# GpSimd issues the direct tiles' stores, the gates' convolution gets a low rank, a third place for sums of values, and sums in DRAM closer together

## The chip, the core and the metric

The kernel runs on one core of one Trainium2 chip. Its time is the device time of one launch in microseconds (us); three launches gave 1119.26, 1120.39 and 1120.42, so the median is 1120.39 us. The core has a matrix engine (PE, with its weight loads shown as PEld), a vector engine (DVE), a scalar engine (ACT), GpSimd (POOL) and a queue engine (SP) that does no arithmetic here but issues nearly all transfers. Each engine runs its own list of instructions in order; an instruction that waits holds up everything behind it on that engine.

## What is computed

One layer of a bidirectional encoder over 256 positions and 16 meta tokens, in float32: two groups of attention heads, an output projection, and then a gated MLP whose gate passes a convolution of width 3 over the positions. The change touches the MLP alone:

```python
def conv_glu(x, w_gate, w_up, conv_w, conv_b, w_down):
    L = x.shape[1]
    g = x @ w_gate
    u = x @ w_up
    pad = CONV_W // 2
    gp = jnp.pad(g, ((0, 0), (pad, pad), (0, 0)))
    gc = conv_b
    for i in range(CONV_W):
        gc = gc + conv_w[i] * gp[:, i:i + L]
    return (jax.nn.silu(gc) * u) @ w_down
...
        h = h + mix @ w_out[l]
        h = h + conv_glu(rmsnorm(h, ffn_norm_g[l]), w_gate[l], w_up[l], conv_w[l], conv_b[l], w_down[l])
    return h[:, N_META:]
```

D_MODEL is 2048 (16 tiles of 128), D_FF is 5632 (44 tiles).

## The kernel before

**Weights.** All weights are float32 and are streamed from DRAM in pieces of up to 128x1024. SP issues the load of a piece into a buffer (`raw`, `more_raw`, and late in the kernel `halves`, which is the same pool of buffers; all loads have line 540). ACT writes a rounded copy of the piece, `whi` (L247), DVE writes the remainder `wlo = raw - whi` (L251), and PE makes each product in parts: the high half of the weights with the high and the low half of the data, and the low half of the weights with the high half of the data (L710 to L712, L2026 and L2027, L287). There are four `whi` and four `wlo` buffers, so DVE can be at most four pieces ahead of PE.

**The MLP** begins about 396 us into the span. Gate and up tiles come in pairs. `gated` (called when a gate tile's products are complete) multiplies by the row's scale and then makes the convolution: one activation on ACT, two SCALAR_TENSOR_TENSOR on DVE (L259), a SiLU on ACT. `tile_up` multiplies the up tile by the gate, and `finish_value` stores the value as two halves in `act`. Five groups of four up tiles (QUADS) are made by a scheme with seven products in place of eight; it needs sums of the data, which for some are kept in `act` (`near`) and for others come from DRAM (`s_up`) into one of two buffers `sin` (the slots `s_parts`), and sums of the weights, which DVE makes. The down projection has three parts: 512 columns by the scheme with narrow products ("mid", `w_down_m`, its sums of values saved in `s_down` and loaded again through `s_parts`), 1024 columns by the scheme with wide products (`w_down_s`), and four tiles of 128 columns made directly (`w_down`). A direct tile has six pieces of up to 8 blocks each. Of its 22 pairs' weight sums the wide part takes one or two of three from DRAM (`early`): GpSimd adds them there with accumulating transfers (L779), between about 400 and 830 us.

**A direct tile's end** (`down_out`): for the first three, ACT copies two halves out of PSUM, GpSimd makes three additions and products (L275), and SP issues the store (L2015), behind whatever GpSimd still has to do. For the last tile DVE makes two operations. `mid_out` and `scheme_out` end the other two parts: DVE combines the seven products, ACT scales, GpSimd adds the residual (L275), SP stores (L2181, L2222).

**The order of everything** is made by a planner in the kernel: each piece of work is a coroutine that asks for an engine with a cost in ns, and `Flow.run` always takes the one that can start first, ties and ranks by `order()` (a lower rank goes first). So a changed cost or rank moves instructions on every engine. The table `work` sets the order of PE's weight pieces; `TAIL` says how the last six pieces of mid ("m") and the first pieces of the direct tiles ("d") alternate before the wide part begins.

Of the kernel before, what the change touches and what calls it, by code (L numbers as in the profile page):

```python
# [34 lines left out]
KC = D_MODEL // P  # L35
# [23 lines left out]


THIRD = 2
MID_SUMS = 0
EARLY_PACE = 18000.0
LANDING = 2600.0
BEHIND = 4
MID_LEAD, TAIL = 4, "mmdmmdddmmddd"
LAST = FC // 2 - 1


# [145 lines left out]
def encoder_block(ctx: ExitStack, tc: tile.TileContext, io):  # L215
# [15 lines left out]
    def size(ap):  # L231
        n = 1
        for s in ap.shape[1:]:
            n *= s
        return n
# [7 lines left out]
    def ACT(out, in_, f, **kw):  # L243
        ns = (51 if in_psum(in_) else 93) + 0.833 * size(in_)
        ns += 93 * (columns(kw.get("scale")) + columns(kw.get("bias")) > 0)
        yield "act", ns + 113 * ("accum_out" in kw)
        nc.scalar.activation(out, in_, f, **kw)  # L247
# [9 lines left out]
    def STT(out, a, s, b, op0, op1):  # L257
        yield "dve", 68 + 62 * columns(s) + 1.04 * size(out)
        nc.vector.scalar_tensor_tensor(out, a, s, b, op0, op1)  # L259
# [11 lines left out]
        nc.vector.reciprocal(out, a)  # L271

    def PTT(out, a, b, op):
        yield "pool", 90 + 2.7 * size(out)
        nc.gpsimd.tensor_tensor(out, a, b, op)  # L275

    def cost(l, r):
# [28 lines left out]
    def one(slots):  # L306
        (t,) = yield slots, 1
        return t
# [1585 lines left out]
    def gated(f, gate):  # L1894

        yield ev_mlp
        gs = yield from one(mts)

        yield from TT(gs[:, : SEQ + 1], gate[:, : SEQ + 1], s_2[:, : SEQ + 1], ALU.mult)
        fl.put(acc, gate)  # L1900
        gc = yield from one(mts)
        g_ = gc[:, :SEQ]
        yield from ACT(
            g_, gs[:, 1 : 1 + SEQ], AF.Identity, scale=vec("conv0", f), bias=vec("conv_b", f)
        )
        yield from STT(g_, gs[:, :SEQ], vec("conv1", f), g_, ALU.mult, ALU.add)
        yield from STT(
            gc[:, 1:SEQ], gs[:, : SEQ - 1], vec("conv2", f), gc[:, 1:SEQ], ALU.mult, ALU.add
        )
        yield from ACT(gs[:, :SEQ], g_, AF.Silu)  # L1910
        fl.put(mts, gc)
        gates[f] = gs
        fl.set(ev_gate[f])
# [50 lines left out]
    def save_sums(dst, saved, parts, release):  # L1964
        yield "sp", 600
        load(dst, parts, saved, nc.sync)
        fl.cur.t = saved.time
        if release:
            fl.put(combined, parts)

# [27 lines left out]
    def down_out(m, ps):  # L1998
        o = yield from one(mts)
        o_ = o[:, :SEQ]  # L2000
        if m < KC - ST - 1:
            t = yield from one(mts)
            yield from ACT(o_, ps[:, :SEQ], AF.Copy)
            yield from ACT(t[:, :SEQ], ps[:, SEQ:], AF.Copy)
            fl.put(acc, ps)
            yield from PTT(o_, t[:, :SEQ], o_, ALU.add)
            fl.put(mts, t)
            yield from PTT(o_, o_, s_2[:, :SEQ], ALU.mult)
            yield from PTT(o_, o_, hT[ST + m][:, :SEQ], ALU.add)
        else:  # L2010
            yield from TT(o_, ps[:, :SEQ], s_2[:, :SEQ], ALU.mult)
            fl.put(acc, ps)
            yield from TT(o_, o_, hT[ST + m][:, :SEQ], ALU.add)
        yield "sp", 600
        nc.sync.dma_start(io["outT"][:, m, :], o_)  # L2015
        fl.cur.t += 4000.0
        fl.put(mts, o)

# [74 lines left out]
    def scheme_products(p, r):  # L2093
        if r.last and not r.wide and p is r.pieces[0]:
            fl.spawn(reserve())
        if r.of != "up":
            yield ev_act[2 * r.g]
            yield ev_act[2 * r.g + 1]
        for i, n in enumerate(p.products):
            if r.first:  # L2100
                yield from sums7_bank(r, n)
            if n in (1, 2, 4):
                k, h = {1: (0, 0), 2: (1, 0), 4: (1, 1)}[n]
                k += 2 * r.g
                A = hl[k] if r.of == "up" else act[:, k]
                a = [A[:, j, h * P : (h + 1) * P] for j in range(2)]
            else:
                yield r.ev_S
                if r.near:
                    r.S = near[r.g]  # L2110
                o = P * {6: 0, 7: 1, 3: 2, 5: 3}[n]
                a = [
                    r.S[:, j * PW // 2 + o : j * PW // 2 + o + P].bitcast(F32R) for j in range(2)
                ]
            t = slice(i * r.q, (i + 1) * r.q)
            for s, ev in zip(p.parts, p.ready):
                if s.start < t.stop:
                    yield ev

            j = r.order.index(n)  # L2120
            start = r.first and (r.wide or j % 2 == 0)
            stop = r.last and (r.wide or j % 2 == 1 or j == 6)
            yield from MM(product3(sums7[n], a, (p.hi[:, t], p.lo[:, t]), start, stop))
        finished()
        if p is r.pieces[-1]:
            if not r.near:
                fl.put(s_parts, r.S)
            elif r.last_near:
                fl.set(ev_far[r.g])
            if r.last:  # L2130
                P7 = dict(sums7)
                sums7.clear()
                if r.of == "down":
                    fl.spawn(scheme_out(P7))
                elif r.of == "mid":
                    fl.spawn(mid_out(r.order, P7, dict(sum_banks)))
                else:
                    fl.spawn(quad_out(r.quad, r.order, P7, dict(sum_banks)))
# [33 lines left out]
    def mid_out(order, P7, b):  # L2172
        out = yield from reserved()
        U = quarters_of(out)
        yield from seven(order, P7, b, U)
        for i in range(2):
            for j in range(2):
                yield from ACT(U[i][j], U[i][j], AF.Copy, scale=s_2t[:, i : i + 1])
                yield from PTT(U[i][j], U[i][j], res[SL // (2 * P) + j][:, i, :], ALU.add)
            yield "sp", 600  # L2180
            nc.sync.dma_start(io["out"][i][:, SL:], out[:, i * SM : (i + 1) * SM])  # L2181
        fl.cur.t += 4000.0
        fl.put(raws, out)

# [26 lines left out]
    def scheme_out(sums7):  # L2211
# [4 lines left out]
        def done(i, j):  # L2216
            for k in range(2):
                o = C[i][j][:, k * 2 * P : (k + 1) * 2 * P]
                yield from ACT(o, o, AF.Copy, scale=s_2t[:, i : i + 1])
                yield from PTT(o, o, res[2 * j + k][:, i, :], ALU.add)  # L2220
            yield "sp", 600
            nc.sync.dma_start(io["out"][i][:, j * SL // 2 : (j + 1) * SL // 2], C[i][j])  # L2222

# [22 lines left out]

    fl.spawn(split_x(), 2)
    fl.spawn(split_hi(), lambda: -1 if 16 < n_split[0] < at[0] + 2 else 2)
    fl.spawn(split_lo(), lambda: -1 if 16 < n_split[1] < at[0] + 2 else 2)
    fl.spawn(square_x(), lambda: 3 if sq_n[0] < 10 else 0)  # L2250
    fl.spawn(sum_x(), 3)
    fl.spawn(scale_x())
# [165 lines left out]
```

## Time and profile before

| what | value |
|---|---|
| three launches | 1119.26, 1120.39, 1120.42 us |
| the profiled execution's own time | 1118.23 us |
| its span | 1116.4 us |
| matmuls | 8164 |
| PE's share of the span | 99% |
| DVE's share | 91% |
| ACT's share | 68% |
| POOL's share | 14% |

The span runs from the first to the last instruction. The busy time of PE is the union of its matmuls, whose ends are modelled and overlap, so a matmul that runs at a lower clock still counts as busy. The granted clock (PEclk) is 1.00 at full speed. In the timeline a row is: start in us, duration in us, engine, line, operation, out<-in, shape, how many were merged, and in brackets the idle time of the engine before it and what ended that.

### The profile page before, as it was taken

To read this page: it belongs to the slowest core of one execution; us is meant where nothing else is said; L and a number is where in the kernel's file an instruction comes from. 1 tells how busy PE (TensorE), PEld (TensorE's weight loads), DVE (VectorE), ACT (ScalarE), POOL (GpSimd) and SP (SyncE) were. 2 spreads that over 40 slices of the span, in tenths; PEclk is the share of its full clock that TensorE was granted. 3 is DMA by queue.
4 is the path that set the end of the run, shared out by engine and by line. 5 is a ranking of instruction groups with operands and counts; after the bars stand their busy time and mean duration, and the time that the engine had idled before them with its cause. 6 is when DMAs were issued, how large, how long until landed. Compare 5 with 4: busy or idle time off the path is not lost.

```text
span 1116.4 us, 22345 instructions
## 1 busy us (share of the span) xinstructions
PE 1099.7 (99%) x8164; PEld 1048.3 (94%) x8164; DVE 1012.1 (91%) x1918; ACT 754.1 (68%) x1518; POOL 157.6 (14%) x216
## 2 busy tenths in 40 slices
PE   9999999999999999999999999999999999998998
PEld 9999999999999999999999999999999999786877
DVE  8979888888879899999999999999999999997996
ACT  8688979897647776556665665665566565665564
POOL 3211222122333400000000000000000000304022
PEclk9999999999999999999999999999999999998999
DMA  8654435344655798787868778898898889797881
GB/s 325 196 167 133 153 111 165 132 149 150 228 182 167 210 335 273 252 244 233 295 193 250 254 245 282 268 284 274 302 345 305 277 302 334 249 333 260 295 302 51
DMA packets 82887, 265.35 MB, mean 238 GB/s; under 512 B 9304, under 2 KB 13400, under 8 KB 82776
## 3 DMA queue, kind: packets, MB, share of 16 engines
q1 hardware_dynamic: 79320, 255.00, 66.4%
q0 software_dynamic: 3168, 8.65, 4.9%
q8 instruction: 64, 1.05, 0.4%
q14 instruction: 47, 0.39, 0.1%
q10 hardware_dynamic: 288, 0.27, 0.1%
HBM read 245.39 MB, written 35.13 MB: 251 GB/s over the span
## 4 chain that ended last, share of the span: by engine, by line
PE 64%; DVE 19%; DMA 7%; ACT 6%; issue 3%; POOL 1%; SPq 0%; DVEq 0%; ACTq 0%; POOLq 0%
PE bank L287 17%; PE bank L712 11%; PE bank L710 11%; PE bank L711 11%; DVE wlo L251 10%; PE bank L2026 7%; PE bank L2027 4%; DVE raw L251 3%; ACT whi L247 3%; DVE mt L251 2%; PE bank L293 2%; DMA s_up<-sums 1%; POOL mt L275 1%; DMA halves<-early 1%; ACT scr L247 1%
## 5 line engine op out<-in xcount | busy, mean ns | idle before, releaser
L247 ACT ACTIVATE whi<-raw 128x512 fp32r<-128x512 f32 (+2 forms) x510 | 383.8, 770 | 164.5 <-PE bank L711 58.0
L251 DVE TENSOR_TENSOR wlo<-raw,whi 128x512 fp32r<-128x512 f32 (+2 forms) x510 | 444.8, 891 | 32.2 <-ACT whi L247 29.5
L710 PE MATMUL bank<-hl,whi 128*128 128x258 f32 (+1 forms) x1208 | 347.8, 288 | 0.1
L712 PE MATMUL bank<-hl,wlo 128*128 128x258 f32 (+1 forms) x1208 | 343.2, 284 | 1.2 <-DVE wlo L251 1.1
L711 PE MATMUL bank<-hl,whi 128*128 128x258 f32 (+1 forms) x1208 | 343.7, 285 | 0.0
L712 PEld LDWEIGHTS bank<-hl,wlo 128*128 128x128 f32 x1208 | 229.7, 190 | 1.9 <-DVE wlo L251 1.8
L711 PEld LDWEIGHTS bank<-hl,whi 128*128 128x128 f32 x1208 | 229.3, 190 | 0.1
L710 PEld LDWEIGHTS bank<-hl,whi 128*128 128x128 f32 x1208 | 228.4, 189 | 0.8 <-ACT scr L247 0.3
L287 PE MATMUL bank<-whi,act 128*128 128x256 f32 (+1 forms) x560 | 146.7, 309 | 0.0
L2026 PE MATMUL bank<-hl,whi 128*128 128x512 f32 x384 | 136.2, 394 | 0.0
L2027 PE MATMUL bank<-hl,wlo 128*128 128x256 f32 x384 | 107.6, 280 | 0.0
L287 PEld LDWEIGHTS bank<-whi,act 128*128 128x128 f32 x560 | 99.5, 190 | 6.2
L287 PE MATMUL bank<-wlo,act 128*128 128x256 f32 (+1 forms) x280 | 86.6, 309 | 0.0
L287 PE MATMUL bank<-whi,sin 128*128 128x256 f32 (+1 forms) x304 | 85.1, 327 | 1.5 <-DMA sin<-s_up 1.5
L2026 PEld LDWEIGHTS bank<-hl,whi 128*128 128x128 f32 x384 | 72.2, 188 | 14.9
L247 ACT ACTIVATE whi<-halves 128x1024 fp32r<-128x1024 f32 (+2 forms) x68 | 61.9, 930 | 34.6 <-PE bank L287 19.3
L779 POOL DMA_DIRECT2D early<-in_w_down_s x22 | 18.1, 825 | 426.2 <-DMA early<-in_w_down_s 410.2
L251 DVE TENSOR_TENSOR wlo<-halves,whi 128x1024 fp32r<-128x1024 f32 (+2 forms) x68 | 72.2, 1088 | 2.7 <-ACT whi L247 2.6
L2027 PEld LDWEIGHTS bank<-hl,wlo 128*128 128x128 f32 x384 | 72.4, 188 | 0.0
L247 ACT ACTIVATE whi<-more_raw 128x1024 fp32r<-128x1024 f32 (+2 forms) x61 | 50.8, 844 | 30.8 <-PE bank L287 13.9
L287 PEld LDWEIGHTS bank<-whi,sin 128*128 128x128 f32 x304 | 53.9, 188 | 7.6 <-ACT mt L247 1.6
L251 DVE TENSOR_TENSOR wlo<-more_raw,whi 128x1024 fp32r<-128x1024 f32 (+2 forms) x61 | 57.7, 957 | 1.2 <-ACT whi L247 1.1
(310 smaller groups left out, 2177.4 us busy)
## 6 DMA issues: line engine op xcount, KB each, us to landing
raw<-in_w_gate SPq DMA_DIRECT2D x75, 512.0 KB, 5.9
raw<-in_w_in SPq DMA_DIRECT2D x52, 512.0 KB, 3.9
raw<-in_w_up SPq DMA_DIRECT2D x40, 512.0 KB, 5.8
sin<-s_down SPq DMA_DIRECT2D x35, 512.0 KB, 6.2
raw<-in_w_out SPq DMA_DIRECT2D x32, 512.0 KB, 3.9
raw<-in_w_up_s SPq DMA_DIRECT2D x32, 512.0 KB, 5.6
s_down<-sums SPq DMA_DIRECT2D x22, 512.0 KB, 6.7
raw<-in_w_down_m SPq DMA_DIRECT2D x16, 512.0 KB, 6.1
```

Of the source, the lines that this page charges most:

```text
L247: nc.scalar.activation(out, in_, f, **kw)
L251: nc.vector.tensor_tensor(out, a, b, op)
L275: nc.gpsimd.tensor_tensor(out, a, b, op)
L287: nc.tensor.matmul(o, l, r, start=start, stop=stop)
L293: nc.tensor.transpose(o, i, ident[:n, :n])
L710: nc.tensor.matmul(ps, whi, xhi, start=start, stop=False)
L711: nc.tensor.matmul(ps, whi, xlo, start=False, stop=False)
L712: nc.tensor.matmul(ps, wlo, xhi, start=False, stop=stop)
L779: nc.gpsimd.dma_start(t, src, accum_op=ALU.add)
L2026: nc.tensor.matmul(ps, whi, x, start=start, stop=False)
L2027: nc.tensor.matmul(ps[:, :n], wlo, x[:, 0, :], start=False, stop=stop)
```

## The change

```diff
 THIRD = 2
+GATE_PRIO = 2
+LENT = 14
 MID_SUMS = 0
-EARLY_PACE = 18000.0
-LANDING = 2600.0
+EARLY_PACE = 15000.0
+LANDING, SAVING = 2600.0, 2500.0
 BEHIND = 4
-MID_LEAD, TAIL = 4, "mmdmmdddmmddd"
+MID_LEAD, TAIL = 4, "mmdmmddddmmdddd"
...
-        yield "pool", 90 + 2.7 * size(out)
+        yield "pool", 90 + (2.7 if fl.cur.t < 4e5 else 3.9) * size(out)
...
         fl.put(acc, gate)
+        fl.spawn(convolved(f, gs), GATE_PRIO)
+
+    def convolved(f, gs):
         gc = yield from one(mts)
...
-        fl.cur.t = saved.time
+        fl.cur.t = saved.time + SAVING
...
-        yield "sp", 600
-        nc.sync.dma_start(io["outT"][:, m, :], o_)
+        if m < KC - ST - 1:
+            yield "pool", 1000
+            nc.gpsimd.dma_start(io["outT"][:, m, :], o_)
+        else:
+            yield "sp", 600
+            nc.sync.dma_start(io["outT"][:, m, :], o_)
...
             if not r.near:
-                fl.put(s_parts, r.S)
+                if r.S is not near[-1]:
+                    fl.put(s_parts, r.S)
+                elif r.g < LENT:
+                    fl.put(s_parts, r.S)
+                else:
+                    fl.set(ev_far[-1])
             elif r.last_near:
-                fl.set(ev_far[r.g])
+                if r.g < KC // 2 - 1:
+                    fl.set(ev_far[r.g])
+                else:
+                    fl.put(s_parts, near[-1])
...
-            yield "sp", 600
-            nc.sync.dma_start(io["out"][i][:, SL:], out[:, i * SM : (i + 1) * SM])
+            yield "pool", 1000
+            nc.gpsimd.dma_start(io["out"][i][:, SL:], out[:, i * SM : (i + 1) * SM])
...
-                yield from ACT(o, o, AF.Copy, scale=s_2t[:, i : i + 1])
-                yield from PTT(o, o, res[2 * j + k][:, i, :], ALU.add)
+                r, s = res[2 * j + k][:, i, :], s_2t[:, i : i + 1]
+                if i:
+                    yield from STT(o, o, s, r, ALU.mult, ALU.add)
+                else:
+                    yield from ACT(o, o, AF.Copy, scale=s)
+                    yield from PTT(o, o, r, ALU.add)
...
-    fl.spawn(split_lo(), lambda: -1 if 16 < n_split[1] < at[0] + 2 else 2)
+    fl.spawn(split_lo(), lambda: -1 if 16 < n_split[1] < at[0] + (2 if at[0] < 100 else 3) else 2)
```

Five stores go from SP's list to GpSimd's: three of the direct tiles and the two of the mid part. The convolution of a gate becomes a thread of its own with rank 2, behind the splits of the weights and the work of rank 0. After the last group of four, the last of the `near` places in `act` serves as a third place for the sums of values of the mid part, up to its pair 14. The sums in DRAM are asked for every 15 us of the planner's clock in place of 18. The planner reckons with slower GpSimd operations after 400 us and with a later release of the buffer of sums. Two direct pieces move from inside the wide part to ahead of it (nine "d" in TAIL, not seven). Half of the wide part's end goes from ACT and GpSimd to DVE (four SCALAR_TENSOR_TENSOR). The low halves are given precedence up to three pieces ahead of PE. All arithmetic that makes a value is the same, apart from the operation that scales and adds at the wide part's end.

Three places where the lists change. Names ending in numbers are buffers; the numbers differ between the two programs. First SP's list in the wide part, before: the loads around the second direct tile's store.

```order
L540 DMA raw_80<-in_w_down_s 128x1024
L540 DMA halves_11043<-in_w_down_s 128x512
L540 DMA sums_93<-s_down_124 128x1024
L2015 DMA outT<-mt_5395 128x256
L540 DMA halves_11164<-early_147 128x1024
L540 DMA halves_11164<-in_w_down_s 128x1024
L540 DMA sin_5398<-s_down_125 128x1024
L540 DMA halves_11086<-early_148 128x512
```

And now:

```order
L542 DMA raw_80<-in_w_down_s 128x1024
L542 DMA halves_11164<-in_w_down_s 128x512
L542 DMA sums_93<-s_down_124 128x1024
L542 DMA halves_11043<-early_147 128x1024
L542 DMA halves_11043<-in_w_down_s 128x1024
L542 DMA sin_5412<-s_down_125 128x1024
L542 DMA raw_82<-early_148 128x512
```

The store of the direct tile is gone from between the loads of pair 11's and pair 12's data; the loads stand in the same order.

Second, GpSimd's list at the same direct tile, now; the two DMA rows are stores that stood in SP's list before.

```order
L277 TENSOR_TENSOR raw_83<-raw_83,resT_5390 128x256
L2198 DMA out<-raw_83 128x512
L277 TENSOR_TENSOR mt_5401<-mt_5407,mt_5401 128x256
L277 TENSOR_TENSOR mt_5401<-mt_5401,s_165 128x256
L277 TENSOR_TENSOR mt_5401<-mt_5401,res_4068 128x256
L2021 DMA outT<-mt_5401 128x256
L277 TENSOR_TENSOR mt_5402<-mt_5403,mt_5402 128x256
```

The stores (L2198 of the mid part, L2021 of the direct tile) now stand behind the arithmetic that they wait for, and ahead of the next direct tile's arithmetic only.

Third, DVE's list in the last group of four up tiles, before: a gate's convolution (L259) and the low halves (`wlo`) of the next pieces.

```order
L251 TENSOR_TENSOR raw_80<-raw_84 128x512
L251 TENSOR_TENSOR raw_80<-raw_84,raw_80 128x256
L251 TENSOR_TENSOR raw_80<-raw_80,raw_84 128x256
L259 SCALAR_TENSOR_TENSOR mt_5393<-mt_5395,vecs,mt_5393 128x256
L259 SCALAR_TENSOR_TENSOR mt_5394<-mt_5396,vecs,mt_5394 128x256
L259 SCALAR_TENSOR_TENSOR mt_5393<-mt_5395,vecs,mt_5393 128x255
L259 SCALAR_TENSOR_TENSOR mt_5394<-mt_5396,vecs,mt_5394 128x255
L251 TENSOR_TENSOR wlo_90<-raw_84,whi_86 128x512
L251 TENSOR_TENSOR wlo_90<-raw_84,whi_86 128x256
L251 TENSOR_TENSOR wlo_91<-raw_83,whi_87 128x1024
```

And now:

```order
L253 TENSOR_TENSOR raw_80<-raw_82,raw_80 128x256
L253 TENSOR_TENSOR raw_80<-raw_80,raw_82 128x256
L253 TENSOR_TENSOR wlo_89<-raw_84,whi_85 128x1024
L253 TENSOR_TENSOR wlo_90<-raw_82,whi_86 128x512
L253 TENSOR_TENSOR wlo_90<-raw_82,whi_86 128x256
L253 TENSOR_TENSOR mt_5401<-bank_73,s_165 128x257
L253 TENSOR_TENSOR mt_5407<-bank_75,s_165 128x257
L253 TENSOR_TENSOR wlo_91<-raw_83,whi_87 128x1024
L261 SCALAR_TENSOR_TENSOR mt_5404<-mt_5401,vecs,mt_5404 128x256
L261 SCALAR_TENSOR_TENSOR mt_5404<-mt_5401,vecs,mt_5404 128x255
```

The low halves of the same weights, and of the gate piece behind them, now stand ahead of the convolution.

## The prediction

> **What bounds the kernel now.** I read first the page's head, then a table of windows by stage, then the stage that loses most, engine by engine.
>
> ```profile
> span 1116.4 us, 22345 instructions
> PE 1099.7 (99%) x8164; PEld 1048.3 (94%) x8164; DVE 1012.1 (91%) x1918; ACT 754.1 (68%) x1518; POOL 157.6 (14%) x216
> ...
> 0.00:396.00 396.00, 393.19 (x3203) 388.55 (x3204) 340.55 (x801) 310.49 (x854) 105.44 (x173) 1.00 0.54 177
> 396.00:945.00 549.00, 545.85 (x4179) 527.14 (x4179) 521.33 (x948) 341.38 (x543) 18.15 (x22) 1.00 0.85 278
> 945.00:1092.00 147.00, 139.84 (x645) 113.37 (x644) 135.92 (x154) 90.87 (x106) 27.54 (x13) 0.98 0.81 281
> 1092.00:1117.00 25.00, 20.86 (x144) 19.20 (x142) 14.31 (x18) 11.31 (x17) 6.51 (x8) 0.98 0.13 48
> ```
>
> In the window rows the columns are length, busy time of PE, PEld, DVE, ACT and POOL, granted clock, DMA share and GB/s. PE sets the time almost everywhere, and the change takes no matmul away. So all that can be won is PE's idle time: 2.8 us before 396, 3.15 in the MLP's first 549 us, 7.16 in the wide part of the down projection (945 to 1092), and 4.1 at the end. In the wide part DVE is hardly less busy (135.92) than PE (139.84), and the granted clock is under 1.00. I cut that part finer.
>
> ```profile
> 1008.00:1020.00 12.00, 12.00 (x57) 9.83 (x56) 9.23 (x11) 7.80 (x9) 11.22 (x3) 1.00 0.43 148
> 1020.00:1026.00 6.00, 0.86 (x4) 0.38 (x2) 2.28 (x3) 0.83 (x2) 0.00 (x0) 0.81 0.90 276
> 1026.00:1034.00 8.00, 7.70 (x26) 6.24 (x27) 7.34 (x10) 3.46 (x4) 0.00 (x0) 0.71 1.04 408
> ```
>
> One hole holds most of it: from 1020 to 1026 PE works 0.86 us, and before it the transfers fall to 148 GB/s. PE's rows at this place, then SP's, POOL's and DVE's:
>
> ```profile
> 1020.47 0.39 PE L287 MATMUL bank<-whi,sums 128*128 128x512 f32 x1
> 1026.30 0.80 PE L287 MATMUL bank<-wlo,sums 128*128 128x512 f32 x1 [5.44 <-DVE wlo L251]
> ...
> 1030.68 0.39 PE L287 MATMUL bank<-whi,act 128*128 128x512 f32 x1
> ...
> 1032.98 0.39 PE L2026 MATMUL bank<-act,whi 128*128 128x512 f32 x1
> 1033.20 0.28 PE L2027 MATMUL bank<-act,wlo 128*128 128x256 f32 x1
> 1033.32 0.40 PE L2026 MATMUL bank<-act,whi 128*128 128x512 f32 x1
> ...
> 1008.39 0.38 SPq L540 DMA_DIRECT2D sums<-s_down  x1
> 1019.40 0.34 SPq L2015 DMA_DIRECT2D outT<-mt  x1
> 1019.85 0.37 SPq L540 DMA_DIRECT2D halves<-early  x1
> ...
> 1006.87 10.96 POOL L275 TENSOR_TENSOR mt<-mt,mt 128x256 f32<-128x256 f32 x1 [47.29 <-ACT mt L247]
> 1017.91 0.75 POOL L275 TENSOR_TENSOR mt<-mt,s 128x256 f32<-128x256 f32 x1
> 1018.74 0.64 POOL L275 TENSOR_TENSOR mt<-mt,res 128x256 f32<-128x256 f32 x1
> ...
> 1016.02 1.22 DVE L251 TENSOR_TENSOR wlo<-raw,whi 128x1024 fp32r<-128x1024 f32 x1
> 1023.69 0.69 DVE L251 TENSOR_TENSOR halves<-raw,halves 128x512 f32<-128x512 f32 x1 [6.46 <-DMA halves<-early]
> ...
> SPq L2015 <- POOL mt L275: 19.1, 3, 10.5
> ```
>
> Read backwards, this is one chain. PE waits 5.44 us for a low half; DVE had been idle 6.46 us for a load (`early`); SP issued that load at 1019.85, right behind a direct tile's store, and had issued nothing since 1008.39; the store waited 10.5 us for GpSimd, whose first operation took 10.96 us where the next two of the same shape took 0.75 and 0.64. It ended 0.6 us after DVE's unbroken row of operations did (1016.02 + 1.22 = 1017.24). Afterwards PE is slow as well: the ten matmuls from 1026.30 to 1030.68 take 4.38 us, the ten from there to 1032.98 take 2.30. So the hole costs 5.44 + 2.08 = 7.5 us.
>
> **The change part by part.**
>
> *The stores.* Three of the direct tiles and two of the mid part leave SP's list. Behind the store at 1019.40 stood loads alone, and nothing on SP waits for GpSimd in the wide part any more. On GpSimd each becomes an issue; the nearest row is its other issue:
>
> ```profile
> L779 POOL DMA_DIRECT2D early<-in_w_down_s x22: 807/812/984, 403.9 to 829.8; - x22
> ```
>
> That is 0.8 us each, 4.1 us for five, on an engine that is busy 27.54 of 147 us. What is queued behind them is the next tile's arithmetic, for which only its own store waits, and the mid part's buffer, which a load takes 18 loads later. So the cost is 0, and the gain 7.5 if the loads then come in time. Bounds: PE cannot win more in this part than its idle time and the slow matmuls, 7.16 + 2.1 = 9.3; DVE's idle time, 147 - 135.92 = 11.1, would allow that. Below, nothing excludes that a new wait takes all of it: 0. That the transfers can keep up is shown by a stage with more traffic and no idle PE:
>
> ```profile
> 720.00:945.00 225.00, 225.00 (x1674) 215.18 (x1673) 211.92 (x373) 137.81 (x215) 4.91 (x6) 1.00 0.89 303
> ```
>
> The wide part moves 147 x 281 = 41.3 MB (in thousands of GB/s x us); in 139.5 us that is 296 GB/s, under 303. I take 7.5, near the row that I can follow through.
>
> The Trainium skill, "SBUF — State Buffer", section "SBUF: two separate sides", says that DVE and GpSimd share a pair of SBUF ports, locked for a whole instruction, when DVE has two SBUF inputs and GpSimd reads SBUF; the 10.96 us beside DVE's unbroken row agree. The same section speaks against the change: a transfer issued by GpSimd needs descriptors that GpSimd writes itself, and it cannot while DVE holds the ports in a two-port mode. The 22 issues above, at 0.8 us beside a DVE busy 521 of 549 us, show no such delay; by the rule the stores would land later, and by the argument above the sum would stay.
>
> *Two direct pieces ahead of the wide part.* A block of a direct piece takes PE 0.34 us (1032.98 to 1033.32), 8 blocks 2.7 us, and DVE one operation of 1.2. So 5.4 us of PE's work and 2.4 of DVE's leave the wide part for the stretch ahead of it, where PE waits for nothing and DVE has 13 us to spare in 225 (211.92). PE's total is the same: 0 by itself. It makes DVE less and PE much less of the wide part, so DVE is nearer to being its bound.
>
> *The gates' convolution.* Where the MLP's first stage loses PE time:
>
> ```profile
> 530.00:536.00 6.00, 5.60 (x45) 5.28 (x45) 5.89 (x11) 5.18 (x10) 0.00 (x0) 1.00 0.92 255
> 655.00:660.00 5.00, 4.29 (x36) 4.08 (x35) 4.78 (x8) 3.31 (x6) 0.00 (x0) 1.00 0.60 198
> 692.00:695.00 3.00, 2.44 (x17) 2.03 (x16) 2.97 (x8) 0.63 (x1) 0.00 (x0) 1.00 0.96 246
> 713.00:718.00 5.00, 3.53 (x30) 3.36 (x29) 5.00 (x10) 3.99 (x7) 0.00 (x0) 1.00 0.94 332
> ...
> 713.12 1.67 DVE L259 SCALAR_TENSOR_TENSOR mt<-mt,vecs,mt 128x256 f32<-128x256 f32 x4
> ...
> PE bank L287 <- DMA sin<-s_up: 1.5, 1, 1.5
> ```
>
> Four places with 0.40, 0.71, 0.56 and 1.47 us, together all of the 3.15. In the fourth the four operations of a convolution (1.67 us) stood ahead of the low halves; they now stand behind. But PE's wait there ended with a load (`sin<-s_up`), so I do not count it. The first and the third are waits for DVE's list (low halves; the combined products of a group of four), where the new order serves: 0.40 + 0.56 = 1.0. Bounds: 3.15 won, or as much lost, since every list in this stage is new. I take 1.0.
>
> *The rest.* The third place for sums, the later release and the higher price of GpSimd change the order only; in the mid part, where the place serves, PE has no idle time to win (225.00 of 225): 0. Sums in DRAM every 15 us in place of 18: the same 22 transfers are done in five sixths of 829.8 - 403.9, ending about 759, so a sixth more of their traffic there and none later; the stage runs at share 0.85 beside the 0.89 above: 0, and the fourth place above says what a late load costs, 1.5. At the end four ACT and four GpSimd operations become four on DVE, 4 x 0.42 by the row at 713.12:
>
> ```profile
> 1112.89 0.42 DVE L251 TENSOR_TENSOR mt<-bank,s 128x256 f32<-128x256 f32 x1 [5.29 <-PE bank L712]
> ```
>
> DVE waits 5.29 us there for PE's last matmul, so 1.7 us more are hidden: 0. Without that cover they would cost 1.7.
>
> **The sum**: 7.5 + 1.0 = 8.5 us. The profiled execution took 1118.23, 1.8 more than its span; it would take 1109.7. The runs' median is 2.2 higher, 1120.4, so 1111.9 is the forecast.
>
> **The rivals.**
>
> *Loads and DVE take the hole over: 1116.4.* For it: also after the hole DVE waits for loads of the same kind.
>
> ```profile
> DVE raw L251 <- DMA raw<-early: 1.7, 1, 1.7
> DVE raw L251 <- DMA halves<-early: 1.1, 1, 1.1
> ```
>
> Both lie in the last 58 us of the wide part, with SP free. At that rate 147 us hold 7.1 of DVE's 11.1, so 4.0 are won, and none elsewhere. Against it: these may be the hole's own echo.
>
> *All waits go: 1108.0.* The wide part's 9.3 and the first stage's 3.15 make 12.4. Against it: one of these waits ended with a load that the change does not hasten.
>
> *The wait comes back: 1119.4.* The mid part's stores hold a buffer that a later load takes, and ahead of them stand seven GpSimd operations. If they are held as long as the one of 10.96, SP stops at that load instead; the stop above cost 7.5, which leaves 1.0 won. Against it: its 18 loads of distance. By the skill's rule on descriptors it would be this one.
>
> *Slower: gates too late, 1125.3.* Rank 2 puts the convolution behind all splits, on a DVE that is busy 95% of the first stage. A group of four holds its PSUM bank until the gate is there, and 12 `mt` buffers are shared; if DVE comes to the convolution only when PE already needs the bank, PE waits for its 1.67 us. There are 22 pairs of gates; from the sixth (6 x 1.67 = 10) it outweighs 8.5; with eight it is 13.4 - 8.5 = 4.9 slower. Against it: in the list the convolution comes one or two pieces later, no more.
>
> **How the numbers follow.** The forecast 0.50, loads and DVE 0.22, all waits 0.13, the wait comes back 0.05, gates too late 0.10. About 0.2% (2.2 us) is what a measurement can tell from no change, so faster 0.85, same 0.05, slower 0.10. The range reaches below 1108.0 by the 1.5 of one late load, 1106.5, and above 1116.4 by 2.1 for the matmuls that would run slowly once more, to 1118.5; outside lie the last two cases.
>
> **What would show it.** Right: SP's list without a stop of over 5 us between 945 and 1090, whatever GpSimd's operations take; no PE wait over 2 us there and a clock of 1.00; PE's idle time in the wide part under 3 us. The order of the first stage is right if the waits at the first and third place are gone. Wrong: PE idle there again, behind DVE waiting for `early` (second case), SP stopped at a load into the buffer of the mid part's stores (fourth), or PE waiting for banks that wait for gates (fifth).

## The result, and the profile after

The changed kernel took 1116.85 us (median of six launches, 1114.51 to 1117.46) beside 1119.83 of the kernel before (six launches): ratio 0.9971, 95% interval [0.9957, 0.9985]. It is faster, inside the range, but by 3.0 us where 8.5 were forecast. In a second sitting (below) the same two kernels gave 1114.72 and 1120.37, ratio 0.9948 [0.9934, 0.9962]. So the gain is 3 to 6 us, and a third to two thirds of the forecast gain did not come.

The profiled execution took 1116.94 us. Its span on the page, and its windows (columns as before):

```profile
span 1114.8 us, 22339 instructions
```

```profile
396.00:945.00 549.00, 545.84 (x4149) 525.52 (x4148) 517.49 (x941) 338.55 (x540) 18.18 (x22) 1.00 0.85 276
945.00:1092.00 147.00, 144.39 (x685) 117.32 (x684) 141.04 (x161) 95.55 (x111) 19.84 (x18) 1.00 0.84 287
```

The wide part is as forecast: PE works 144.39 of 147 us (139.84 before), at a clock of 1.00 (0.98), and gets 685 matmuls done where it had done 645. But look at the row above it. PE's busy time in the 549 us is the same as before to 0.01 us (545.84 and 545.85), and yet it did 4149 matmuls there, not 4179. The busy time hides the loss, because matmuls that run slowly count as busy, and so does a short pause: at full speed a matmul of 0.28 us starts every 0.12.

So stages are better measured by the starts of matmuls that both programs have: the first with 512 columns (just before the MLP), the last with 258 columns (the end of the gate and up tiles), the last with 512 columns (the end of the wide part). Every trace has 3,656 matmuls of 128x258 and 978 of 128x512. From the timeline of before:

```profile
389.94 0.48 PE L2026 MATMUL bank<-hl,whi 128*128 128x512 f32 x1
...
908.14 0.28 PE L712 MATMUL bank<-hl,wlo 128*128 128x258 f32 x1
...
1099.51 0.39 PE L287 MATMUL bank<-whi,sin 128*128 128x512 f32 x1
```

and of the changed kernel:

```profile
390.75 0.39 PE L2035 MATMUL bank<-hl,whi 128*128 128x512 f32 x1
...
912.55 0.28 PE L714 MATMUL bank<-hl,wlo 128*128 128x258 f32 x1
...
1097.40 0.39 PE L289 MATMUL bank<-whi,sin 128*128 128x512 f32 x1
```

The gate and up tiles took 518.20 us before and 521.80 now: 3.6 us lost. The rest up to the last wide matmul took 191.37 and now 184.85: 6.5 won. At the same landmark at 390, before the MLP, the changed kernel was already 0.8 late, and from the last wide matmul to the span's end it takes 17.4 in place of 16.9. Together -6.5 + 3.6 + 0.8 + 0.5 = -1.6, which is the difference of the spans.

What took the hole's place? At the second direct tile GpSimd now has its turn at once, and its issue of the store costs 0.57 us:

```profile
999.43 1.49 POOL L277 TENSOR_TENSOR mt<-mt,mt 128x256 f32<-128x256 f32 x1 [30.07 <-ACT mt L249]
...
1004.05 0.57 POOL L2021 DMA_DIRECT2D outT<-mt  x1 [0.41 <-POOL mt L277]
```

In the wide part PE and DVE wait for this (waits: engine and line, what for, us in total, times, longest):

```profile
PE bank L289 <- DVE wlo L253: 1.6, 4, 0.6
PE bank L2036 <- DVE wlo L253: 0.9, 1, 0.9
...
DVE wlo L253 <- ACT whi L249: 3.9, 5, 1.5
DVE halves L253 <- DMA halves<-early: 0.7, 1, 0.7
DVE more_raw L253 <- DMA halves<-early: 0.7, 1, 0.7
```

No PE wait is over 0.9 us, and only 1.4 us of DVE's idle time ends with a load of `early`.

The largest loss of the gate and up tiles lies in one place; PE's other waits of this stage are 0.3 us and less. PE's, DVE's and ACT's rows there, then two windows:

```profile
660.10 0.38 PE L289 MATMUL bank<-whi,act 128*128 128x256 f32 x1 [0.62 <-ACT whi L249]
661.36 0.39 PE L289 MATMUL bank<-wlo,act 128*128 128x256 f32 x1 [0.88 <-DVE wlo L253]
...
662.89 0.42 PE L712 MATMUL bank<-hl,whi 128*128 128x258 f32 x1
...
666.09 0.28 PE L712 MATMUL bank<-hl,whi 128*128 128x258 f32 x1
...
654.77 0.81 DVE L253 TENSOR_TENSOR mt<-mt,mt 128x128 f32<-128x128 f32 x3
655.62 0.29 DVE L253 TENSOR_TENSOR mt<-mt 128x128 f32<-128x128 f32 x1
655.94 0.62 DVE L253 TENSOR_TENSOR mt<-mt,mt 128x128 f32<-128x128 f32 x2
656.48 0.69 DVE L253 TENSOR_TENSOR raw<-raw 128x512 f32<-128x512 f32 x1
...
660.08 2.96 DVE L253 TENSOR_TENSOR wlo<-raw,whi 128x1024 fp32r<-128x1024 f32 x3 [1.18 <-ACT whi L249]
...
658.99 2.00 ACT L249 ACTIVATE whi<-raw 128x1024 fp32r<-128x1024 f32 x2 [4.57 <-DVE raw L253]
```

```profile
653.00:666.00 13.00, 11.22 (x75) 10.40 (x74) 11.59 (x22) 5.74 (x9) 0.00 (x0) 0.87 0.78 247
660.00:666.00 6.00, 5.02 (x27) 4.83 (x28) 5.89 (x9) 3.30 (x6) 0.00 (x0) 0.72 0.64 218
```

Six small sums (`mt`) stand ahead of the sums of weights on DVE; ACT waits 4.57 us for these sums before it can round them; DVE then waits 1.18 for ACT's `whi`, and PE for both. Afterwards 15 matmuls, from 662.89 to 666.09, take 3.20 us, 0.21 each in place of 0.12, at a granted clock of 0.72. In before the same 13 us had 102 matmuls, where here there are 75:

```profile
653.00:666.00 13.00, 12.29 (x102) 12.08 (x102) 12.71 (x24) 8.57 (x14) 0.00 (x0) 1.00 0.77 260
```

### The profile page after: what moved, and what is told of

Its sections match the earlier page's. It is cut to its first block, busy times and chain, and to the rows that moved or that the text cites. A ratio compares the mean times of both kernels' runs of the same rounds, so it can differ in the third digit from the quotient of the medians.

```text
span 1114.8 us, 22339 instructions
## 1 busy us (share of the span) xinstructions
PE 1102.8 (99%) x8164; PEld 1049.1 (94%) x8164; DVE 1015.9 (91%) x1922; ACT 751.8 (67%) x1514; POOL 142.8 (13%) x217
## 4 chain that ended last, share of the span: by engine, by line
PE 62%; DVE 21%; DMA 7%; ACT 5%; issue 4%; POOL 0%; SPq 0%; DVEq 0%; ACTq 0%; POOLq 0%
PE bank L289 14%; DVE wlo L253 12%; PE bank L714 11%; PE bank L712 11%; PE bank L713 11%; PE bank L2035 8%; PE bank L2036 4%; DMA raw<-in_w_up_s 3%; ACT whi L249 3%; DVE raw L253 2%; PE bank L295 2%; DVE mt L253 2%; DMA halves<-early 1%; DVE halves L253 1%; DVE mt L261 1%
## 5 line engine op out<-in xcount | busy, mean ns | idle before, releaser
L289 PE MATMUL bank<-whi,act 128*128 128x256 f32 (+1 forms) x600 | 153.2, 306 | 0.6 <-ACT whi L249 0.6
L289 PEld LDWEIGHTS bank<-whi,act 128*128 128x128 f32 x600 | 105.1, 189 | 7.0 <-ACT whi L249 0.8
L289 PE MATMUL bank<-wlo,act 128*128 128x256 f32 (+1 forms) x300 | 92.3, 308 | 1.4 <-DVE wlo L253 1.4
L249 ACT ACTIVATE whi<-halves 128x1024 fp32r<-128x1024 f32 (+1 forms) x68 | 63.7, 948 | 32.3 <-PE bank L289 17.5
L253 DVE TENSOR_TENSOR wlo<-halves,whi 128x1024 fp32r<-128x1024 f32 (+1 forms) x68 | 74.1, 1113 | 4.2 <-ACT whi L249 4.2
L289 PE MATMUL bank<-whi,sin 128*128 128x256 f32 (+1 forms) x264 | 76.6, 333 | 0.0
L289 PEld LDWEIGHTS bank<-wlo,act 128*128 128x128 f32 x300 | 56.7, 189 | 5.3 <-DVE wlo L253 2.2
```

The source lines that it names most:

```text
L253: nc.vector.tensor_tensor(out, a, b, op)
L289: nc.tensor.matmul(o, l, r, start=start, stop=stop)
```

## The experiments

Two questions: is it the moved stores that closed the hole, and what of the change costs the 3.6 us? The table gives each kernel's median, its ratio to the kernel before on the same chip with its 95% interval (taken over all executions, so it is not quite the ratio of the medians), and the stage times of its one profiled execution by the landmarks above: S1 from the first 512-column matmul to the last 258-column one, S2 from there to the last 512-column one, end from there to the end of the span.

| kernel | median us | ratio | S1 | S2 | end |
|---|---|---|---|---|---|
| before (profile above) | 1119.83 | 1 | 518.2 | 191.4 | 16.9 |
| changed | 1116.85 | 0.9971 [0.9957, 0.9985] | 521.8 | 184.9 | 17.4 |
| after_again: changed, second sitting | 1114.72 | 0.9948 [0.9934, 0.9962] | 521.2 | 185.5 | 17.4 |
| stores_alone | 1113.77 | 0.9945 [0.9928, 0.9962] | 519.3 | 185.4 | 17.4 |
| after_stores_sp | 1114.94 | 0.9958 [0.9937, 0.9978] | 521.4 | 185.7 | 16.9 |
| gates_alone | 1124.03 | 1.0033 [1.0015, 1.0052] | 520.0 | 192.3 | 16.9 |
| after_gates_rank0 | 1115.78 | 0.9964 [0.9946, 0.9983] | 522.9 | 184.3 | 17.4 |
| after_pace18 | 1113.66 | 0.9949 [0.9933, 0.9965] | 521.8 | 185.1 | 17.4 |
| after_lo2 | 1114.11 | 0.9944 [0.9927, 0.9962] | 520.4 | 184.0 | 17.4 |
| after_saving0 | 1114.23 | 0.9949 [0.9933, 0.9965] | 522.1 | 184.0 | 17.4 |
| tail_alone | 1112.46 | 0.9948 [0.9924, 0.9973] | 518.9 | 185.2 | 16.9 |
| mix | 1113.73 | 0.9942 [0.9928, 0.9956] | 521.2 | 184.2 | 17.4 |
| mix_no_third | 1111.75 | 0.9922 [0.9907, 0.9937] | 517.8 | 183.4 | 17.4 |
| after_no_third | 1115.54 | 0.9958 [0.9946, 0.9969] | 520.9 | 185.4 | 17.5 |

**The stores alone.** The kernel before, its order kept, with the five stores issued by GpSimd:

```diff
-        nc.sync.dma_start(io["outT"][:, m, :], o_)
+        (nc.gpsimd if m < KC - ST - 1 else nc.sync).dma_start(io["outT"][:, m, :], o_)
...
-            nc.sync.dma_start(io["out"][i][:, SL:], out[:, i * SM : (i + 1) * SM])
+            nc.gpsimd.dma_start(io["out"][i][:, SL:], out[:, i * SM : (i + 1) * SM])
```

> The kernel before, with one edit: the five stores are issued by GpSimd at the same places of the plan; PE's, DVE's and ACT's lists are word for word those of before, SP's list lacks the five rows. Theory H (the stop of SP behind the second store cost 5.44 us of PE and 2.08 us of slow matmuls, and goes with the store): 5 to 7.5 us faster than before (ratio 0.9933 to 0.9955), no stop of SP over 5 us between 945 and 1090, granted clock 1.00 there, and the idle time of PE in the first stage of the MLP (396 to 945) unchanged at about 3.15 us. Rival (loads and DVE take the hole over): at most 4 us faster (ratio 0.9964 or more), PE idle again in the wide part behind DVE waiting for loads of early.

GpSimd's rows, and a window over the place where the hole was:

```profile
1008.05 11.56 POOL L275 TENSOR_TENSOR mt<-mt,mt 128x256 f32<-128x256 f32 x1 [46.38 <-ACT mt L247]
...
1022.74 0.57 POOL L2015 DMA_DIRECT2D outT<-mt  x1 [0.41 <-POOL mt L275]
```

```profile
1016.00:1026.00 10.00, 10.00 (x47) 7.84 (x46) 9.93 (x11) 6.29 (x8) 6.75 (x4) 1.00 0.83 276
```

GpSimd is held as long as before (11.56 us), its store is issued only at 1022.74, and PE works all of the 10 us. So the chain of the prediction holds: what cost the time was that the loads stood behind the store. S2 falls by 6.0, with the rest of the kernel as it was.

**The changed kernel with the stores back on SP.**

```diff
-            nc.gpsimd.dma_start(io["outT"][:, m, :], o_)
+            nc.sync.dma_start(io["outT"][:, m, :], o_)
...
-            nc.gpsimd.dma_start(io["out"][i][:, SL:], out[:, i * SM : (i + 1) * SM])
+            nc.sync.dma_start(io["out"][i][:, SL:], out[:, i * SM : (i + 1) * SM])
```

> The changed kernel, with the five stores issued by SP at the same places of the plan, all else in the same order. Theory H (the stores are what was won, the new order of the rest lost about 3 us): 5 us or more slower than the changed kernel, so 1119 to 1125 us, ratio to before 0.999 to 1.005, with a stop of SP of several us behind a store. Rival (the wide part was healed by its new order and the two direct pieces ahead, not by the stores): as fast as the changed kernel, ratio 0.997.

GpSimd's first operation of the second direct tile, the window of the wide part, and a row of SP's waits in it:

```profile
997.94 1.51 POOL L277 TENSOR_TENSOR mt<-mt,mt 128x256 f32<-128x256 f32 x1 [30.95 <-ACT mt L249]
```

```profile
945.00:1092.00 147.00, 143.46 (x680) 116.55 (x679) 139.94 (x159) 96.01 (x111) 16.13 (x13) 1.00 0.83 286
```

```profile
SPq L2198 <- POOL raw L277: 6.0, 2, 5.8
```

The hole does not come back. In the new order GpSimd's operation takes 1.51 us, so this store is not late, wherever it is issued. The stop of SP that H named does appear, 5.8 us behind a store of the mid part (L2198), but it costs little: S2 is 185.7, beside 184.9 and 185.5 of the changed kernel. The moved stores cure the old order; in the changed kernel they cure nothing that was still there.

**Two direct pieces ahead, alone.** Which part of the new order did it? The kernel before with one table changed, all stores on SP:

```diff
-MID_LEAD, TAIL = 4, "mmdmmdddmmddd"
+MID_LEAD, TAIL = 4, "mmdmmddddmmdddd"
```

> The kernel before with two more direct pieces ahead of the wide part and nothing else; all stores stay on SP. Theory 'the wide part was cured twice: DVE has less to do there, so GpSimd gets its turn and SP's store is not late': GpSimd's first operation of the second direct tile takes 1 to 3 us, SP has no stop of over 5 us, the hole of 5.44 us is gone; ratio 0.9945 to 0.996. Rival 'the hole goes only where the rest of the order is new as well': that operation still takes about 10 us, the hole stays within 1 us of 5.4, the ratio is 0.999 to 1.001.

The same operation, a window around it, and a row of SP's waits in the wide part:

```profile
995.28 1.01 POOL L275 TENSOR_TENSOR mt<-mt,mt 128x256 f32<-128x256 f32 x1 [31.46 <-ACT mt L247]
```

```profile
994.00:1000.00 6.00, 5.90 (x25) 4.22 (x24) 6.00 (x5) 4.78 (x7) 4.12 (x3) 1.00 0.98 344
```

```profile
SPq L2181 <- POOL halves L275: 5.2, 2, 5.1
```

In this execution the table alone closes the hole: S2 falls by 6.2, and the ratio is that of the stores alone. SP still stops once for 5.1 us behind a store of the mid part, and no hole follows. The reason that was written down with it, that DVE has less to do there, is not borne out: DVE works 6.00 of 6.00 us while GpSimd gets its turns. The direct tile ends 12 us earlier, and GpSimd is not held there; why stays open.

Nor is it the same in every execution. Six of this kernel's eight took 1111.59 to 1113.00 us, at a granted clock of 1.000 over the whole execution. The other two took 1119.59 and 1121.51 at 0.996 and 0.995, like the kernel before, whose clock the slow matmuls behind the hole lower to 0.997. And of the 76 executions of the kernel before whose clock is on record, four took 1112.17 to 1114.62 at 1.000, as if the hole were not there. No profile of these six was kept, so that GpSimd was held in the two and not in the four is inferred from time and clock. With the stores alone all ten executions lie between 1112.68 and 1115.58. So the table makes the hole rarer, and the moved stores make a held GpSimd harmless.

**The gates' rank, alone and taken back.** Alone, in the kernel before; and the changed kernel with rank 0:

```diff
+        fl.spawn(convolved(f, gs), 2)
+
+    def convolved(f, gs):
```

> The kernel before, with one edit: the convolution of a gate is a thread of rank 2. Theory G (the low rank brings the value sums of two pairs together on DVE ahead of the weights' sums, which costs PE 2 to 4 us between 580 and 670, slow matmuls among them): 1 to 4 us slower than before, ratio 1.001 to 1.0035, PE idle time in 396 to 945 of 4 us or more counted with slow matmuls. Rival (as predicted: it takes away 1.0 us of waits): ratio 0.998 to 1.000.

```diff
-GATE_PRIO = 2
+GATE_PRIO = 0
```

> The changed kernel with rank 0 for the convolution. Theory G: 2 to 4 us faster than the changed kernel, 1113 to 1115 us, ratio to before 0.994 to 0.996, and no cluster of waits near 653 to 666. Rival (another part of the change, such as the denser sums in DRAM, makes the waits there): 1116 to 1118 us, ratio 0.996 to 0.999.

Alone it is slower by 1.0033 [1.0015, 1.0052]; S1 grows by 1.8 us, and the hole stays (5.37 us, behind a GpSimd operation of again 10.96). The loss is not where G put it: of six PE waits of over 0.3 us in S1, one lies between 580 and 670. From its timeline, and from PE's waits between 396 and 945 us, where the row for low halves had 1.1 us in before:

```profile
1008.94 10.96 POOL L275 TENSOR_TENSOR mt<-mt,mt 128x256 f32<-128x256 f32 x1 [47.29 <-ACT mt L247]
...
1028.30 0.79 PE L287 MATMUL bank<-wlo,sums 128*128 128x512 f32 x1 [5.37 <-DVE wlo L251]
```

```profile
PE bank L712 <- DVE wlo L251: 2.6, 5, 0.8
```

But taking the rank back does not repair S1 (522.9), and the waits near 658 us stay, as the rival said. The rank costs something in the old order, and is not what costs in the new one.

**Three other parts, each taken back in the changed kernel:** the pace of the sums in DRAM, the low halves' precedence, the later release of the sums' buffer.

```diff
-EARLY_PACE = 15000.0
+EARLY_PACE = 18000.0
```

> The changed kernel with the sums in DRAM asked for every 18 us of the planner's clock again. Theory P (the denser sums bring the loads of the up tiles' scheme later in the plan and fill DVE's list with other work ahead of the weights' sums; this is the loss between 580 and 700): the excess of PE between 580 and 700 falls from 7 to 2 or 3 us, time 1112 to 1114 us, ratio to before 0.992 to 0.995. Rival (the precedence of the low halves or the later release of the buffer of sums makes it): excess of 5 us or more there, with the waits near 658 again, ratio 0.996 to 0.998.

```diff
-    fl.spawn(split_lo(), lambda: -1 if 16 < n_split[1] < at[0] + (2 if at[0] < 100 else 3) else 2)
+    fl.spawn(split_lo(), lambda: -1 if 16 < n_split[1] < at[0] + 2 else 2)
```

> The changed kernel with the low halves given precedence up to two pieces ahead of PE throughout, as before. Theory Lo (low halves of gate pieces three ahead go before the weights' sums, whose piece PE then waits for; this is the loss between 580 and 700): the excess of PE between 580 and 700 falls from 7 to 2 or 3 us, ratio to before 0.992 to 0.995. Rival (denser sums or later release): excess of 5 us or more there, ratio 0.996 to 0.998.

```diff
-LANDING, SAVING = 2600.0, 2500.0
+LANDING, SAVING = 2600.0, 0.0
```

> The changed kernel with the planner's release of the buffer of sums at the landing of its store, as before. Theory S (the 2.5 us later release sets the value sums of two pairs side by side on DVE, ahead of the weights' sums; this is the loss between 580 and 700): the excess of PE between 580 and 700 falls from 7 to 2 or 3 us, ratio to before 0.992 to 0.995. Rival (denser sums or the precedence of the low halves): excess of 5 us or more there, ratio 0.996 to 0.998.

Each removes the waits near 658 us, as written down, and each gets others, which was not; with the old pace PE waits 2.59 us at a place where neither kernel had waited:

```profile
458.77 0.58 PE L714 MATMUL bank<-hl,wlo 128*128 128x258 f32 x1 [2.59 <-DVE wlo L253]
```

S1 is 521.8, 520.4 and 522.1. The three ratios cannot be told from that of the changed kernel in its second sitting (0.9948), so none of these parts carries the loss.

**The changed kernel again, and the late parts without the new first stage.** If no single part owns the loss, the new order as a whole should. The mix is the kernel before with the stores on GpSimd, the two direct pieces ahead, the end's four SCALAR_TENSOR_TENSOR and the third place for sums; the other kernel leaves out the third place, so that its lists are those of before up to about 855 us.

> The changed kernel itself once more, beside the kernel before and the three that follow, so that they are compared in one sitting. If its own order of the first stage costs more than the re-planned ones with one part taken back (ratios 0.9944 to 0.9949), its ratio is again near 0.997; if its first six times were merely high, it comes out at 0.9945 to 0.9955 and no order of the first stage among those tried is better than another by more than a run's scatter.

> The kernel before, with only those parts of the change that leave the lists as they were up to about 750 us: the five stores on GpSimd, two more direct pieces ahead of the wide part, four SCALAR_TENSOR_TENSOR at the end, the third place for sums. Theory 'the first stage's new order is what is lost': PE's waits up to 750 us are those of before and the wide part loses about 5, as in the changed kernel or in the kernel with the stores alone; ratio 0.992 to 0.995, about 1113, below the changed kernel's. Rival 'the lost microseconds come from the late parts (two pieces ahead, third place)': waits of over 1 us appear between 750 and 1000 us, and the ratio is 0.996 or more, above the 0.9945 of the stores alone.

> As the mix of late parts, without the third place for sums, so the lists are those of before up to about 855 us. Theory 'the third place and the later release are worth nothing, since PE waits for nothing between 720 and 945 us': within 1.5 us of the mix. Rival 'the third place takes loads out of the wide part': slower than the mix by 2 us or more, with more waits for loads between 945 and 1092 us.

The changed kernel's ratio, 0.9948, is the one that was written down for the case that its first six times were merely high; part of the 3.0 to 5.6 us between the sittings is such scatter. But its S1 came out as in its first profile (521.2), with the two waits again (the matmuls behind them start at 658.30 and 659.55), and the other half of that case, that no order of the first stage is better than another, does not hold: the kernel with the late parts and without the third place is the fastest of all, 1111.75 us, 3.0 under the changed kernel in the same sitting. The two profiles put the gain where the theory has it, S1 517.8 against 521.2, and 2.1 us more in S2. DVE's waits in the wide part, of the kernel with the two direct pieces alone:

```profile
DVE wlo L251 <- ACT whi L247: 3.6, 5, 1.5
DVE halves L251 <- DMA raw<-early: 1.2, 2, 0.9
DVE raw L251 <- DMA halves<-early: 1.2, 1, 1.2
```

and of the mix without the third place, where no wait ends with a load of `early` any more:

```profile
DVE wlo L251 <- ACT whi L247: 4.3, 7, 1.5
DVE halves L251 <- issue: 0.4, 1, 0.4
```

Of the third place both cases missed: without it the mix is 2.0 us faster, which is more than "worth nothing" allowed and has the other sign than "takes loads out of the wide part". The mix with it shows the rival's sign, a new wait between 750 and 1000 us, though its ratio is the one of the theory. Its windows and the rows there:

```profile
820.00:824.00 4.00, 4.00 (x29) 3.67 (x27) 0.10 (x1) 0.06 (x2) 0.00 (x0) 1.00 1.02 405
824.00:828.00 4.00, 1.82 (x12) 1.61 (x11) 3.93 (x8) 2.16 (x6) 0.00 (x0) 0.87 0.93 376
```

```profile
820.49 0.56 SPq L540 DMA_DIRECT2D act<-s_down  x1
823.90 0.69 DVE L251 TENSOR_TENSOR raw<-raw 128x512 f32<-128x512 f32 x1 [4.40 <-DMA raw<-in_w_down_m]
...
826.70 0.39 PE L712 MATMUL bank<-hl,wlo 128*128 128x258 f32 x1 [2.18 <-DVE wlo L251]
```

DVE does 0.10 us of work from 820 to 824 while the transfers run at a share of 1.02: it waits 4.40 us for a weight piece, and PE then 2.18 for DVE. The piece was issued at 819.52 and used 4.4 us later; in the mix without the third place the same piece was issued at 821.01 and used 2.7 us later. The load into the third place (`act`) was issued in the middle of this, at 820.49; that it delayed the piece is likely, and not tried by itself.

**Is the third place, then, the cost in the changed kernel too?** The changed kernel without it:

```diff
-                if r.g < KC // 2 - 1:
-                    fl.set(ev_far[r.g])
-                else:
-                    fl.put(s_parts, near[-1])
+                fl.set(ev_far[r.g])
```

> The changed kernel without the third place for sums of values. Theory 'the third place changed nothing but the order, and what it costs depends on the order it meets': the waits of the first stage up to 750 us stay where they are (657 and 658 us), the time from the first matmul of 512 columns at 390 us to the last of 258 columns stays within 1.5 us of the 521.2 to 521.8 of the changed kernel, and the ratio is 0.994 to 0.997. Rival 'the third place is what costs the re-planned orders their 3 us, as it cost the mix of late parts 2': that time falls to 518 to 519.3, as in the kernels with the old order, and the ratio is 0.991 to 0.993.

No: S1 is 520.9, the two waits are there (matmuls at 659.17 and 660.43), the ratio is 0.9958. The first theory held.

## Why the prediction was right and wrong

**What bounds the kernel: right.** PE's idle time was the thing to win, and the chain store, load, low half, PE was real; with the stores alone GpSimd is as slow as ever and the hole is gone.

**The stores: right, 7.5 forecast, 6.5 measured in S2** (6.0 with the stores alone). That GpSimd's issue costs nothing was right but for 0.5 us at the very end (below). What the text did not see is that the same change closes the hole a second time.

**Two direct pieces ahead: the step was wrong, though its term did no harm.** I took 0, "PE's total is the same". Alone they give 0.9948 [0.9924, 0.9973], as much as the stores, since in most executions the moved end of the direct tile finds GpSimd free to run. The two cures hardly add, as the hole can be closed once: S2 falls by 6.0 and 6.2 with one of them, and by 8.0 in the mix without the third place, which has both.

**The gates' convolution and the new lists: the step that failed.** I took 1.0 won: I named four places where the first stage waited, found that the new order serves two of them, and counted these. Both waits are indeed gone, as PE's busy time around the two places shows:

```profile
525.00:535.00 10.00, 10.00 (x85) 10.00 (x85) 9.84 (x18) 5.64 (x10) 0.84 (x1) 1.00 0.79 236
...
690.00:700.00 10.00, 10.00 (x66) 9.03 (x65) 9.42 (x16) 5.99 (x9) 0.08 (x1) 1.00 1.04 361
```

But the new order has waits elsewhere, and S1 grew by 3.6 us, just past the bound of 3.15 "or as much lost" that I had set and not used. This term is off by 4.6, and with the 1.0 of the stores, the 0.5 at the end and 0.8 at the landmark at 390 us, which the change doesn't explain (389.4 to 390.8 in the fourteen profiles), it accounts for 6.9 of the 7.2 us between the profiled execution forecast (1109.7) and the one taken (1116.94). The other 0.3 lie outside the span, where 2.1 us pass in place of 1.8.

Most of it is an effect of the order and not one execution's accident: the four profiles with the old lists in this stage have S1 from 517.8 to 519.3, the eight of the changed kernel and its variants 520.4 to 522.9. About 1.6 us of the 3.6 is the slow stretch at 663 us, which the same waits bring in some executions only (last section). Three of the eight have no slow stretch in this stage, and their 520.4, 520.9 and 521.4 still lie above all the old ones. The loss belongs to no single part among the rank, the pace, the precedence, the release and the third place. Why nearly every re-planned order should be worse than the old one is not settled. What the traces show is that DVE has little room there in either order: it is busy 517.49 of 549 us now and was 521.33 before. That every order must therefore leave some waits is argued, not shown.

**The rest at 0.** The four operations at the end are hidden, as forecast: the stores back on SP keep them, and the end is 16.9 as before. The third place is worth nothing in the changed kernel and costs 2 us in the mix.

**The profiled execution and the median.** I added 2.2 us because the profiled execution of before lay that much under its median. The changed kernel's lay on its median (1116.94, 1116.85). The addition was scatter, and it hid part of the miss.

**The rivals.** "Loads and DVE take the hole over: 1116.4" has nearly the measured time, and is wrong: S2 won 6.5, not 4.0, and only 1.4 us of DVE's waits there end with `early`. The loss was in another stage. "All waits go" fell with the first stage. "The wait comes back" did not happen: SP stops at no load for a GpSimd store. The rule on descriptors that the prediction named for it speaks of a two-port mode; no trace here shows whether DVE ran in one, and the issue and landing of these stores show no delay (last section). "Gates too late" had the right direction for its stage, and alone it does make the kernel slower, but not by its mechanism: PE waits for low halves and rounded weights, not for banks.

**The tests that I named.** PE's idle time in the wide part is under 3 us (2.61), its clock 1.00, no wait over 2 us: right. "SP's list without a stop of over 5 us" was a bad test. SP now waits up to 7.9 us for `wlo`, that is for a buffer to come free when it is ahead of DVE, and this costs nothing:

```profile
SPq L542 <- DVE wlo L253: 83.4, 57, 7.9
```

"The order of the first stage is right if the waits at the first and third place are gone" was worse: they are gone, and the stage is slower.

## What to carry to other kernels

A change that makes a planner lay out a stage anew is to be priced by the whole stage, and with both signs: waits that are seen to go say nothing about those that come. Take the parts that leave the tuned lists alone and drop the rest: here the late parts alone give 1111.75 us, 3.0 less than the full change in the same sitting. Look at the times of all executions beside the one that was profiled: with the two direct pieces alone the profile shows no hole, and two executions of eight seem to have it. Measure a stage between matmuls that both programs have, since PE's busy time stayed the same to 0.01 us while the stage lost 3.6.

## What the runs showed of the hardware

**GpSimd can be held through a dozen DVE operations, or not at all.** Its first operation of the second direct tile took 10.96 us in before, 11.56 with the stores alone and 10.96 with the rank alone, each time beside an unbroken row of twelve or thirteen DVE operations. In all three it ended 0.6 us after that row did, although with the stores alone DVE's next operation began only 0.04 us after the row. In the other eleven profiles it took 0.73 to 1.51, with the two direct pieces alone beside a DVE without a gap as well, and executions of one and the same kernel seem to differ. The Trainium skill, "SBUF — State Buffer", section "SBUF: two separate sides", says that whichever of the two starts first has the shared ports for the whole instruction, and the other fully blocks. One DVE operation beside the 10.96 us is at most 1.22 us long, so by that a wait of one operation would be expected; the prediction took the 10.96 us as agreeing, but they span twelve. What decides between the two cases stays open. GpSimd's own issues of transfers were not held: 0.56 to 0.63 us. Nor did these stores land later: 2.3 to 7.3 us after their issue in the changed kernel, and 2.0 to 7.3 with the same stores on SP.

**The same short waits lower the clock in one execution and not in the next.** PE's waits of 0.62 and 0.88 us in the changed kernel were followed by matmuls at half speed, and so were those of its second profile. With the stores back on SP the same two waits were followed by none. Its two rows, and then a window of the changed kernel and the same window of the kernel with the stores on SP:

```profile
659.63 0.39 PE L289 MATMUL bank<-whi,act 128*128 128x256 f32 x1 [0.61 <-ACT whi L249]
660.89 0.38 PE L289 MATMUL bank<-wlo,act 128*128 128x256 f32 x1 [0.87 <-DVE wlo L253]
```

```profile
655.00:668.00 13.00, 11.46 (x79) 10.86 (x78) 11.57 (x23) 6.20 (x9) 0.54 (x1) 0.87 0.76 251
655.00:668.00 13.00, 11.52 (x92) 10.91 (x91) 11.61 (x22) 6.53 (x10) 0.82 (x1) 1.00 0.74 239
```

Five profiles have these two waits. Two of them get 79 and 78 matmuls done in this window at a clock of 0.87, three get 92, 92 and 91 done at 1.00: 13 matmuls of 0.12 us, 1.6 us. The Trainium skill, "TensorE: Matmul & The Clock Gate", section "HAM oscillation — how this bites in real kernels", gives the rule as no idle gaps over about 3.4 us; no single gap here is a third of that.

**The kernel's end is 0.5 us longer where GpSimd issues the stores.** From the last wide matmul to the end of the span it is 16.9 us in the four profiles without such stores and 17.4 to 17.5 in the ten with them, also where the end's operations are those of before. In every trace SP runs at its end a row of nine instructions that wait for semaphores, one every 0.06 us when nothing holds them. In the four the one that waits for the last store is the ninth, in the ten it is the fourth, so five more follow it: 0.3 us. The store, issued by SP in all of them, also lands 1.9 to 2.0 us after its issue in place of 1.7; why it does stays open.
